# The pairs of four heads combined before the other four heads are chosen, in a fused encoder layer with retrieved experts

## The chip, the cores and the metric

The program runs on 1 core of one Trainium2 chip. The metric is the device time of one execution in microseconds (us). Three executions of the kernel before took 3947.78, 3959.03 and 3949.66 us; their median is 3949.66 us. Five engines work beside each other, each through its own list of instructions: PE multiplies matrices, DVE is the vector engine, ACT applies functions, POOL is GpSimd, and SP issues transfers. POOL issues the gathers.

## The reference, cut to what matters

One layer over 1024 tokens of width 1024: RWKV-7 time mixing and chunk-causal attention are added to `x`, then comes a product-key retrieval (PEER), then a gated input embedding and a last norm. The change lies in the retrieval:

```
q = (xb @ w_q).reshape(t, 8 heads, 2, 128)
s = einsum('thcd,hcnd->thcn', q, sub_keys)            # 128 scores for each half of each head
top_s, top_i = top_k(s, 16)                           # the choice: 16 of 128, twice for each head
cand_s = top_s[:, :, 0, :, None] + top_s[:, :, 1, None, :]       # 16 x 16 pairs
cand_i = top_i[:, :, 0, :, None] * 128 + top_i[:, :, 1, None, :]
best_s, best_pos = top_k(cand_s, 16)                  # 16 pairs of each head
idx  = take_along_axis(cand_i, best_pos)              # 8 heads x 16 = 128 experts of a token
gate = softmax(best_s)
act  = gelu(einsum('td,thkd->thk', xb, u_tab[idx]))
out  = einsum('thk,thkd->td', gate * act, v_tab[idx])
```

## The kernel before

The 1024 tokens are 8 blocks of 128 (a block's tokens lie on the 128 partitions), worked in 4 slices of two blocks. For each slice the program has `project_rwkv`, `rwkv` (a serial recurrence in chunks of 64 tokens), `project_rest`, `attend` and `select`. `select` (L753) forms the layer's sum, normalises it and multiplies with the query weights in 16 steps `i`, two for each head: ACT and POOL split a weight tile into two parts (L804, recorded as L282), PE multiplies (L806), PE multiplies with the keys (L813), ACT copies the scores to a tile `s` (L815, five buffers), and DVE chooses 16 of 128 for both blocks (`top16`, L821). After the 16 steps `combine` (L830) runs once for each of the two blocks, for all 8 heads: it adds the pairs of scores (`cs`, 9 instructions at L843) and of indices (`ci`, 11 instructions at L848), chooses 16 of the 50 pairs that can win (`top16` again), looks their indices up (`eq`, L864 to L867), writes the index tile `idx` in two halves of four heads (L869) and the softmax into `gate` (L871 to L876).

`gather` (L891) then works through the 128 experts of each token: for each `k`, POOL issues a gather of one row of `u` for each of the 128 tokens (L900, 128 rows of 4 KB), and DVE multiplies it with the token's input and sums (L902). Such an instruction on DVE is called a row product here; there are 1024 of them, 128 for each of the 8 blocks. In the first part of the program four buffers hold gathered rows (`row`, L882), later seven. The experts' second half is done for blocks 0 to 4 by a dense product over the whole table `v` (`expand` writes one-hot weights, `dense` multiplies) and for blocks 5 to 7 by gathers again (`add_rows`). `ple` and the last norm end the program.

No order is written out by hand. `everything` (L1064) gives each stage a number; a list scheduler fixes the order of each engine's list when the program is built, lower numbers first, by its own estimate of when operands are ready. `gather` has the numbers 50 to 53, most slices' stages lower ones, so row products fill places in which DVE would wait by that estimate. On the chip each engine keeps to that order.

Of the kernel before, what the change touches and what calls it, by code (L numbers as in the profile page):

```python
# [8 lines left out]
F = mybir.dt.float32  # L9
R = mybir.dt.float32r  # L10
I32 = mybir.dt.int32
# [140 lines left out]
class Program:  # L152
# [435 lines left out]
    def chunk_pre(self, pool, psum, B):  # L588
# [8 lines left out]
        halves = (slice(0, 64), slice(64, 128))  # L597
        G, V = [], []
        for c in range(2):
# [3 lines left out]
            for j in range(4):  # L603
# [10 lines left out]
                nc.scalar.activation(vs[:, j], ps[:, 384:448], AF.Copy)  # L614
            G.append(gs)
            V.append(vs)

        def level(l):
            m = t([128, 8, 64], "lm", 2)
            for c in range(2):  # L620
                self.aux.tensor_tensor(m[:, 4 * c:4 * c + 4], G[c][:, :, 0, 0:64],  # L621
                                       self.c("lmask")[:, None, l * 64:l * 64 + 64].to_broadcast([128, 4, 64]), op=OP.mult)
# [10 lines left out]
        for l in range(1, 6):  # L633
# [11 lines left out]
            nc.vector.tensor_tensor(xt, xt, d, op=OP.add)  # L645
        return G, V, xt

# [105 lines left out]
    def select(self, hf, side="left"):  # L753
        nc = self.nc
        bl = SLICES[hf]
        NB, N = len(bl), len(bl) * 128
        ts = self.tile(self.kp, [128, NB, 8, 2, 16], F, "ts", 1)
        ti = self.tile(self.kp, [128, NB, 8, 2, 16], U32, "ti", 1)
        with ExitStack() as s2:
            pool = self.pool(s2, "se", side)  # L760
            psum = self.pool(s2, "sp", side, True)
            t, bank = self.makers(pool, psum)
            y = t([128, 8, N], "act")
            for k in range(8):
                nc.sync.dma_start(y[:, k], self.yg[hf][k] if k < 4 else self.oT[hf][k - 4])
            xs = self.blocks(pool, self.rows("x"), bl)
            m = t([128, 8, N], "act")
            for d in range(8):
                ys = []
                for i, src in enumerate(("rw_wo", "mla_wo")):  # L770
                    w = self.weights(self.wp, self.I[src][d], 4)
                    ps = bank([128, N])
                    self.mm(ps, w, (y[:, 4 * i:4 * i + 4],), 4)
                    gt = t([128, N], "gate", 4)
                    nc.sync.dma_start(gt, self.zT[hf][20 + 8 * i + d])
                    nc.vector.tensor_tensor(gt, gt, ps, op=OP.mult)
                    ys.append(gt)
                self.aux.tensor_tensor(m[:, d], ys[0], ys[1], op=OP.add)
            acc = [bank([128, 512], *(("mm",) if i < 3 else ("tr", 1))) for i in range(2 * NB)]
            for k in range(8):  # L780
                w = self.tile(self.wp, [128, 8, 128], F, "w", WBUF).rearrange("p a n -> p (a n)")
                nc.sync.dma_start(w, self.I["w_out"][k * 128:k * 128 + 128])
                for b in range(NB):
                    for n in range(2):
                        nc.tensor.matmul(acc[2 * b + n], m[:, k, b * 128:b * 128 + 128], w[:, n * 512:n * 512 + 512],  # L785
                                         start=k == 0, stop=k == 7)
            for b, x in enumerate(xs):
                for n in range(2):
                    xd = x[:, n * 512:n * 512 + 512]
                    nc.vector.tensor_tensor(xd, xd, acc[2 * b + n], op=OP.add)  # L790
            for b, x in zip(bl, xs):
                nc.sync.dma_start(self.x1[b], x)
            gf = t([128, 8, N], "act").rearrange("p a b -> p (a b)")[:, :D]
            nc.sync.dma_start(gf, self.I["gffn"].to_broadcast([128, D]))
            rs = self.row_rstd(pool, xs, "n")
            for b, x in zip(bl, xs):
                nc.vector.scalar_tensor_tensor(x, x, rs[:, b - bl[0]:b - bl[0] + 1], gf, op0=OP.mult, op1=OP.mult)
                nc.sync.dma_start(self.h2[b], x)
            hT = [t([128, 8, N], "act", 2, R) for _ in range(2)]
            self.to_T(bank, xs, hT)  # L800
            for i in range(16):
                raw, = self.weights(self.wp, self.I["w_q"][i], 8)
                w = [t([128, 8, 128], n, 1, R) for n in (("whi", "wlo") if i % 2 == 0 else ("x0", "x1"))]
                self.split_to(w, raw, nc.gpsimd)  # L804
                ps = bank([128, N])
                self.mm(ps, w, hT, 8)  # L806
                q = t([128, N], "gate", 4)
                nc.scalar.activation(q, ps, AF.Copy)
                keys = t([128, 128], "keys", 3)
                nc.sync.dma_start(keys, self.I["keys"][:, i])  # L810
                ps = bank([128, NB, 128], "tr", 1)
                for b in range(NB):
                    nc.tensor.matmul(ps[:, b], q[:, b * 128:b * 128 + 128], keys, start=True, stop=True)  # L813
                s = t([128, NB, 128], "s", 5)
                nc.scalar.activation(s, ps, AF.Copy)  # L815
                for b in range(NB):
                    self.top16(s[:, b], ts[:, b, i // 2, i % 2], ti[:, b, i // 2, i % 2])
        for b in range(NB):
            self.combine(bl[b], self.kp, ts[:, b], ti[:, b])

    def top16(self, s, v, i):  # L821

# [4 lines left out]
        nc.vector.max(v[:, 8:16], s)  # L827
        nc.vector.max_index(i[:, 8:16], v[:, 8:16], s)

    def combine(self, b, xp, ts, ti):  # L830


        nc = self.nc
        G = 8
        t = lambda shape, tag, dt=F: self.tile(xp, shape, dt, tag, 1)
        tif = t([128, G, 2, 16], "tif")
        nc.vector.tensor_copy(tif, ti)
        cs, ci = t([128, G, 50], "cs"), t([128, G, 50], "ci", I16)
        o = 0
        bc = lambda x, n: x if x.shape[2] == n else x.to_broadcast([128, G, n])  # L840
        for i0, i1, j0, j1 in [(i, i + 1, 0, 16 // (i + 1)) for i in range(8)] + [(8, 16, 0, 1)]:
            n = (i1 - i0) * (j1 - j0)
            nc.vector.tensor_tensor(cs[:, :, o:o + n], bc(ts[:, :, 0, i0:i1], n), bc(ts[:, :, 1, j0:j1], n), op=OP.add)  # L843
            o += n
        o = 0
        for i0, i1, j0, j1 in RUNS:
            n = (i1 - i0) * (j1 - j0)
            nc.vector.scalar_tensor_tensor(ci[:, :, o:o + n], bc(tif[:, :, 0, i0:i1], n), 128.0,  # L848
                                           bc(tif[:, :, 1, j0:j1], n), op0=OP.mult, op1=OP.add)
            o += n  # L850
        bs, bp = t([128, G, 16], "bs"), t([128, G, 16], "bp", U32)
        idx = self.idx[b] = self.tile(self.sel, [128, 128], I32, f"idx{b}", 1)
        gate = self.gate[b] = self.tile(self.sel, [128, 128], F, f"gate{b}", 1)
        idf = t([128, G, 16], "idf")
        iv = idx.rearrange("p (g k) -> p g k", k=16)
        for g in range(G):
            self.top16(cs[:, g], bs[:, g], bp[:, g])
            for k0, n, m in ((0, 20, 4), (8, 50, 2)):
                if (g + 1) % m:
                    continue  # L860
                hs, ks = slice(g + 1 - m, g + 1), slice(k0, k0 + 8)
                sh = [128, m, 8, n]
                eq = self.tile(xp, [128, D], I16, "eq", 1)[:, :m * 8 * n].rearrange("p (g k n) -> p g k n", g=m, k=8)
                nc.vector.tensor_tensor(eq, bp[:, hs, ks, None].to_broadcast(sh),  # L864
                                        self.c("cand")[:, None, None, :n].to_broadcast(sh), op=OP.is_equal)
                nc.vector.tensor_tensor(eq, eq, ci[:, hs, None, :n].to_broadcast(sh), op=OP.mult)
                nc.vector.tensor_reduce(idf[:, hs, ks], eq, axis=AX.X, op=OP.add)  # L867
            if g % 4 == 3:
                nc.vector.tensor_copy(iv[:, g - 3:g + 1], idf[:, g - 3:g + 1])  # L869
        gv = gate.rearrange("p (h k) -> p h k", k=16)  # L870
        nc.vector.tensor_tensor(gv, bs, bs[:, :, 0:1].to_broadcast([128, G, 16]), op=OP.subtract)  # L871
        nc.scalar.activation(gv, gv, AF.Exp)
        sm = t([128, G], "sm")
        nc.vector.tensor_reduce(sm, gv, axis=AX.X, op=OP.add)
        nc.vector.reciprocal(sm, sm)
        nc.vector.tensor_tensor(gv, gv, sm[:, :, None].to_broadcast([128, G, 16]), op=OP.mult)  # L876
# [244 lines left out]
```

## Time and profile before

| | us |
|---|---|
| median of three executions | 3949.66 (3947.78 to 3959.03) |
| the profiled execution | 3942.72, span of its instructions 3940.7 |
| DVE busy | 3193.8 (81%) |
| PE busy | 3087.6 (78%) |
| POOL busy | 2050.4 (52%) |
| ACT busy | 1276.9 (32%) |

The profile is of one execution; times in it count from its first instruction. An engine's busy time says how long it worked, the waits say what ended its idle times, and the 40 digits of a line show the busy share of equal slices of the span, in tenths. A mean over the whole span mixes stages with different limits, so the stages are read one by one, in windows.

### The profile page before, as it was taken

To read this page: it belongs to the slowest core of one execution; us is meant where nothing else is said; L and a number is where in the kernel's file an instruction comes from. 1 tells how busy PE (TensorE), PEld (TensorE's weight loads), DVE (VectorE), ACT (ScalarE), POOL (GpSimd) and SP (SyncE) were. 2 spreads that over 40 slices of the span, in tenths; PEclk is the share of its full clock that TensorE was granted. 3 is DMA by queue.
4 is the path that set the end of the run, shared out by engine and by line. 5 is a ranking of instruction groups with operands and counts; after the bars stand their busy time and mean duration, and the time that the engine had idled before them with its cause. 6 is when DMAs were issued, how large, how long until landed. Compare 5 with 4: busy or idle time off the path is not lost.

```text
span 3940.7 us, 62191 instructions
## 1 busy us (share of the span) xinstructions
PE 3087.6 (78%) x21999; PEld 2517.8 (64%) x21999; DVE 3193.8 (81%) x6931; ACT 1276.9 (32%) x2723; POOL 2050.4 (52%) x1638
## 2 busy tenths in 40 slices
PE   7998778678879794878866687568888889989581
PEld 7885767666668673578735567446666667767351
DVE  2532888767899685899878778998999999999997
ACT  3231222133222174222138867522221222222341
POOL 0201456645654533576454425446767776666754
PEclk9998899888989796888967788779999999999796
DMA  6236598899868998878888998799999999999986
GB/s 200 88 112 200 183 321 286 285 318 309 313 188 309 322 323 285 305 243 279 311 276 284 302 336 274 233 321 341 386 384 371 390 379 372 373 385 352 329 279 232
DMA packets 502327, 1160.48 MB, mean 294 GB/s; under 512 B 54016, under 2 KB 228352, under 8 KB 502016
## 3 DMA queue, kind: packets, MB, share of 16 engines
q0 software_dynamic: 202752, 738.29, 52.7%
q1 hardware_dynamic: 281984, 402.48, 30.3%
q10 hardware_dynamic: 17280, 15.74, 1.2%
q8 instruction: 174, 2.85, 0.3%
q14 instruction: 137, 1.12, 0.1%
HBM read 1071.38 MB, written 84.93 MB: 293 GB/s over the span
## 4 chain that ended last, share of the span: by engine, by line
DVE 23%; PE 23%; issue 20%; DMA 17%; POOL 10%; ACT 5%; SPq 2%; POOLq 0%; DVEq 0%; ACTq 0%
DVE u L902 9%; DMA u<-in_u_dram,idx 9%; PE mm L290 7%; POOL u L900 6%; POOL u L915 4%; PE mm L785 2%; DVE oa L959 2%; PE w L961 1%; PE inv L586 1%; PE acc L997 1%; DMA u<-in_v_dram,idx 1%; DMA raw<-zT 1%; PE acc L998 1%; PE mm L292 1%; SPq L964 1%
## 5 line engine op out<-in xcount | busy, mean ns | idle before, releaser
L900 POOL DMA_INDIRECT u<-in_u_dram,idx x1024 | 1230.5, 1202 | 1182.1 <-DVE dots L902 625.2
L902 DVE CUSTOM_DVE_ANT_0 u<-u,gh 128x1024 f32<-128x1024 f32 x1024 | 1320.8, 1303 | 226.8 <-DMA u<-in_u_dram,idx 210.1
L915 POOL DMA_INDIRECT u<-in_v_dram,idx x384 | 485.7, 1265 | 230.6 <-DVE x L917 104.1
L290 PE MATMUL mm<-hT,w 128*128 128x128 f32 x4608 | 568.4, 284 | 11.8 <-DMA raw<-zT 3.5
L997 PE MATMUL acc<-vlo,Whi 128*128 128x512 f32 x1280 | 521.8, 408 | 67.4 <-DVE vlo L282 66.8
L290 PEld LDWEIGHTS mm<-hT,w 128*128 128x128 f32 x4608 | 553.1, 199 | 27.6 <-ACT z L326 7.8
L998 PE MATMUL acc<-vhi,Wlo 128*128 128x512 f32 x1280 | 513.4, 401 | 0.0
L996 PE MATMUL acc<-vhi,Whi 128*128 128x512 f32 x1280 | 374.3, 402 | 101.8 <-ACT vhi L280 83.0
L996 PEld LDWEIGHTS acc<-vhi,Whi 128*128 128x128 f32 x1280 | 244.9, 193 | 176.5 <-ACT vhi L280 93.1
L997 PEld LDWEIGHTS acc<-vlo,Whi 128*128 128x128 f32 x1280 | 248.4, 194 | 147.1 <-DVE vlo L282 96.7
L917 DVE SCALAR_TENSOR_TENSOR x<-u,gate,x 128x1024 f32<-128x1024 f32 x256 | 329.2, 1286 | 6.0 <-DMA u<-in_v_dram,idx 2.1
L280 ACT ACTIVATE vhi<-vr 128x512 fp32r<-128x512 f32 x256 | 158.8, 628 | 532.2 <-DMA vr<-in_v_dram 347.6
L961 PE MATMUL w<-ob,oa 128*128 128x128 f32 x1280 | 225.3, 334 | 98.1 <-ACT ob L955 53.5
L961 PEld LDWEIGHTS w<-ob,oa 128*128 128x128 f32 x1280 | 203.6, 240 | 124.9 <-ACT ob L955 81.6
L998 PEld LDWEIGHTS acc<-vhi,Wlo 128*128 128x128 f32 x1280 | 249.1, 195 | 51.6
L959 DVE TENSOR_SCALAR oa<-cst,pt 128x128 f32<-128x128 f32 x640 | 210.7, 388 | 39.3 <-PE w L961 34.8
L954 ACT ACTIVATE ob<-cst,pt 128x128 f32<-128x128 f32 x640 | 204.3, 396 | 0.6 <-PE w L961 0.5
L282 DVE TENSOR_TENSOR vlo<-vr,vhi 128x512 fp32r<-128x512 f32 x256 | 174.7, 693 | 8.0 <-ACT vhi L280 7.9
L280 ACT ACTIVATE Whi<-wr 128x1280 fp32r<-128x1280 f32 x64 | 81.5, 1273 | 287.0 <-PE acc L997 257.6
L917 DVE SCALAR_TENSOR_TENSOR gh<-u,gate,gh 128x1024 f32<-128x1024 f32 x128 | 167.9, 1311 | 4.9 <-DMA u<-in_v_dram,idx 3.0
L290 PE MATMUL mm<-act,w 128*128 128x256 f32 x512 | 134.0, 417 | 45.2 <-DMA act<-yg 29.1
L621 POOL TENSOR_TENSOR lm<-gs,cst 128x256 f32<-128x256 f32 x96 | 100.1, 1063 | 100.9 <-DVE gs L612 56.6
(331 smaller groups left out, 5511.6 us busy)
## 6 DMA issues: line engine op xcount, KB each, us to landing
w<-in_w_in_dram SPq DMA_DIRECT2D x144, 512.0 KB
vr<-in_v_dram SPq DMA_DIRECT2D x256, 256.0 KB
W<-ws SPq DMA_DIRECT2D x40, 1024.0 KB
wr<-W SPq DMA_DIRECT2D x64, 640.0 KB
w<-in_w_q_dram SPq DMA_DIRECT2D x64, 512.0 KB
w<-in_w_out_dram SPq DMA_DIRECT2D x32, 512.0 KB
u<-in_u_dram,idx POOLq DMA_INDIRECT x1024, 6.9
x<-in_x_dram SPq DMA_DIRECT2D x16, 512.0 KB
```

The lines of the kernel that those rows point to most:

```text
L280: self.nc.scalar.activation(act[0], x, AF.Copy)
L290: mm(ps, w[0][:, i], a[0][:, i], start=first, stop=last)
L900: nc.gpsimd.indirect_dma_start(out=u[:], out_offset=None, in_=self.I["u"], in_offset=bass.IndirectOffsetOnAxis(ap=idx[:, k:k + 1], axis=0))
L902: nc.vector.tensor_tensor_reduce(out=u[:], in0=u[:], in1=h[:], scale=1.0, scalar=0.0, op0=OP.mult, op1=OP.add, accum_out=dots[:, k:k + 1])
L915: nc.gpsimd.indirect_dma_start(out=v[:], out_offset=None, in_=self.I["v"], in_offset=bass.IndirectOffsetOnAxis(ap=idx[:, k:k + 1], axis=0))
L917: nc.vector.scalar_tensor_tensor(x, v, gate[:, k:k + 1], x, op0=OP.mult, op1=OP.add)
L954: nc.scalar.activation(c[:, i], self.c("iota"), AF.Abs, bias=pt[:, 1, k + i:k + i + 1])
L959: nc.vector.tensor_scalar(a, self.c("iota"), pt[:, 0, k:k + 1], pt[:, 2, k:k + 1], op0=OP.is_equal, op1=OP.mult)
L961: nc.tensor.matmul(ps[:, i], a, c[:, i], start=True, stop=True)
L996: nc.tensor.matmul(acc[b], wh, vh, start=i == 0, stop=False)
L997: nc.tensor.matmul(acc[b], wh, vl, start=False, stop=False)
L998: nc.tensor.matmul(acc[b], wl, vh, start=False, stop=i == G - 1)
```

## The change

`combine` handles four heads at a call instead of eight. It is called twice in each `select`: after step `i` = 7 for heads 0 to 3 of both blocks, and after step 15 for heads 4 to 7. Both calls write parts of the same `idx` and `gate` tiles.

```diff
@@ select
                 nc.scalar.activation(s, ps, AF.Copy)
                 for b in range(NB):
                     self.top16(s[:, b], ts[:, b, i // 2, i % 2], ti[:, b, i // 2, i % 2])
-        for b in range(NB):
-            self.combine(bl[b], self.kp, ts[:, b], ti[:, b])
+                if i % 8 == 7:
+                    hs = slice(i // 2 - 3, i // 2 + 1)
+                    for b in range(NB):
+                        self.combine(bl[b], self.kp, ts[:, b, hs], ti[:, b, hs], hs)
@@ combine
-    def combine(self, b, xp, ts, ti):
+    def combine(self, b, xp, ts, ti, heads):
...
-        G = 8
+        G = 4
...
-        idx = self.idx[b] = self.tile(self.sel, [128, 128], I32, f"idx{b}", 1)
-        gate = self.gate[b] = self.tile(self.sel, [128, 128], F, f"gate{b}", 1)
+        if b not in self.idx:
+            self.idx[b] = self.tile(self.sel, [128, 128], I32, f"idx{b}", 1)
+            self.gate[b] = self.tile(self.sel, [128, 128], F, f"gate{b}", 1)
+        idx, gate = self.idx[b], self.gate[b]
         idf = t([128, G, 16], "idf")
-        iv = idx.rearrange("p (g k) -> p g k", k=16)
+        iv = idx.rearrange("p (g k) -> p g k", k=16)[:, heads]
...
-        gv = gate.rearrange("p (h k) -> p h k", k=16)
+        gv = gate.rearrange("p (h k) -> p h k", k=16)[:, heads]
```

Lines behind L818 stand 2 to 4 lines lower in the changed kernel (the gather is L904, the row product L906, the write of the indices L873). In the order of the engines the whole list behind the first `select` is made anew. Three places are shown.

DVE at the first row product of the program, before: the first half of block 0's indices is written (L869), and the first row products (L902, written to `u` and `dots`) stand between the look-ups (`eq`, `idf`) of the remaining heads.

```order
L869 CAST idx_995_4356<-idf_4358 128x64
L864 TENSOR_TENSOR eq_4402<-bp_4355,cst_60 128x800
L866 TENSOR_TENSOR eq_4402<-eq_4402,ci_4333 128x800
L867 TENSOR_REDUCE idf_4358<-eq_4402 128x2x8
L864 TENSOR_TENSOR eq_4416<-bp_4355,cst_60 128x640
L902 ISA u_4535,dots_4534<-u_4535,gh_4532 128x1024
```

The same place after the change (L873 writes the indices, L906 is the row product; `s_4352`, `s_4402` and `s_4452` are the scores of the last three steps, `bp` and `cs` belong to block 1's first heads):

```order
L873 CAST idx_931_3954<-idf_3956 128x64
...
L826 MAX ts_3218<-s_4452 128x8 x2
L829 MAX bs_4020<-cs_3998 128x8 x4
L829 MAX ts_3218<-s_4352 128x8 x2
L828 MATCH_REPLACE s_4402<-ts_3218,s_4402 128x128 x2
L827 MAX_INDEX ti_3219<-ts_3218,s_4452 128x8 x2
L830 MAX_INDEX bp_4021<-bs_4020,cs_3998 128x8 x4
L875 TENSOR_TENSOR gate_944_4023<-bs_4020 128x64
L830 MAX_INDEX ti_3219<-ts_3218,s_4352 128x8 x2
L829 MAX ts_3218<-s_4402 128x8 x2
L906 ISA u_4601,dots_4600<-u_4601,gh_4598 128x1024
L828 MATCH_REPLACE s_4452<-ts_3218,s_4452 128x128 x2
```

The first row product now stands among the last choices from 128 scores, in front of the end of three of them; before, all choices lay ahead of it.

POOL at its first gather, after the change: the two splits of the last two steps (`wlo`, `x`), and behind them the gathers.

```order
L282 TENSOR_TENSOR x_992_4317<-w_4314,x_991_4316 128x1024
L282 TENSOR_TENSOR wlo_4367<-w_4364,whi_4366 128x1024
L282 TENSOR_TENSOR x_1008_4417<-w_4414,x_1007_4416 128x1024
L904 DMA u_4601<-in_u_dram,idx_931_3954 128x1024
L904 DMA u_4604<-in_u_dram,idx_931_3954 128x1024
```

Before, the same place reads alike with L900: in both lists all 16 splits of the first `select` stand ahead of the first gather, so nothing moved there.

DVE in the recurrence of the second slice, at the end of its last chunk but one (`us` and `hs` are steps of a chunk, `H` its state), before:

```order
L663 COPY us_7087<-seq_7078 128x256
L902 ISA u_1155_4933,dots_4923<-u_1155_4933,gh_4921 128x1024
...
L902 ISA u_4936,dots_4923<-u_4936,gh_4921 128x1024
...
L667 TENSOR_TENSOR hs_7106<-seq_7089,H_7031 128x256
L902 ISA u_4939,dots_4923<-u_4939,gh_4921 128x1024
...
L669 TENSOR_TENSOR H_7108<-hs_7106,er_6279 128x256
```

and after the change:

```order
L663 COPY us_7153<-seq_7144 128x256
L906 ISA u_5026,dots_4989<-u_5026,gh_4987 128x1024
...
L906 ISA u_5029,dots_4989<-u_5029,gh_4987 128x1024
...
L667 TENSOR_TENSOR hs_7172<-seq_7155,H_7097 128x256
L669 TENSOR_TENSOR H_7174<-hs_7172,er_6345 128x256
```

One row product fewer stands between the same steps. Over the whole list of DVE, the number of row products that stand ahead of the same instruction is counted from the two orders:

| instruction on DVE | its start before, us | row products ahead, before | after |
|---|---|---|---|
| last choice of the first `select` begins | 440 | 0 | 0 |
| first mixing step of the second slice's `rwkv` | 559 | 34 | 54 |
| last query product of its `project_rest` | 682 | 81 | 99 |
| first mask of the second `attend` | 820 | 140 | 146 |
| first choice of the second `select` | 1072 | 230 | 238 |
| first indices of the second slice written | 1191 | 256 | 256 |
| last query product of the third slice | 1278 | 288 | 294 |
| first gated product of the third `select` | 1565 | 396 | 407 |
| first choice of the third `select` | 1708 | 441 | 449 |
| last query product of the fourth slice | 1938 | 519 | 523 |
| first gated product of the fourth `select` | 2279 | 656 | 662 |
| first choice of the fourth `select` | 2421 | 693 | 700 |
| first addition of `dense` | 2630 | 741 | 750 |

## Rows read from the trace of the kernel before

**Rows 1.** The page: engines' busy time, slices of the span, the chain.
```profile
PE 3087.6 (78%) x21999; PEld 2517.8 (64%) x21999; DVE 3193.8 (81%) x6931; ACT 1276.9 (32%) x2723; POOL 2050.4 (52%) x1638
...
DVE 2532888767899685899878778998999999999997
...
DVE 23%; PE 23%; issue 20%; DMA 17%; POOL 10%; ACT 5%; SPq 2%; POOLq 0%; DVEq 0%; ACTq 0%
```

**Rows 2.** Stretches: length, each engine's busy time and instructions, clock, DMA.
```profile
core 0: us, PE busy (x) PEld busy (x) DVE busy (x) ACT busy (x) POOL busy (x), PEclk, DMA share, GB/s
387.00:417.00 30.00, 28.44 (x231) 27.68 (x232) 19.84 (x130) 13.34 (x26) 19.98 (x9) 1.00 0.51 159
417.00:443.00 26.00, 20.32 (x166) 19.56 (x164) 19.48 (x133) 8.23 (x17) 11.18 (x5) 1.00 0.40 134
443.00:518.00 75.00, 56.64 (x464) 54.00 (x464) 71.36 (x261) 12.83 (x29) 27.50 (x24) 0.84 0.75 276
518.00:559.00 41.00, 21.64 (x157) 20.06 (x158) 27.61 (x57) 14.54 (x31) 20.19 (x19) 0.79 0.88 303
...
682.00:820.00 138.00, 90.38 (x1265) 79.80 (x1259) 94.93 (x170) 22.48 (x44) 81.50 (x73) 0.79 0.84 284
...
1072.00:1278.00 206.00, 172.68 (x1809) 155.76 (x1810) 198.50 (x644) 49.04 (x95) 105.77 (x83) 0.93 0.75 248
...
1708.00:1938.00 230.00, 191.13 (x2088) 173.53 (x2085) 225.06 (x684) 56.16 (x106) 143.98 (x106) 0.90 0.82 274
...
2421.00:2630.00 209.00, 120.38 (x711) 108.26 (x709) 202.44 (x682) 97.82 (x224) 88.74 (x66) 0.76 0.80 262
2630.00:3171.00 541.00, 476.51 (x1952) 370.99 (x1951) 503.93 (x812) 121.67 (x167) 371.09 (x277) 0.97 0.98 371
```

**Rows 3.** Combining in order of time on DVE: start, length of all, count.
```profile
444.44 1.27 DVE L848 SCALAR_TENSOR_TENSOR ci<-tif 128x64 int16<-128x64 f32 x11
```

**Rows 4.** Line L843: count, shortest/median/longest in ns.
```profile
L843 DVE TENSOR_TENSOR cs<-ts x72: 149/181/439, 440.3 to 2561.5; 128x16 f32<-128x16 f32 x24, 128x64 f32<-128x64 f32 x16, 128x40 f32<-128x40 f32 x8, 128x32 f32<-128x32 f32 x8
```

**Rows 5.** Lines by group, 443 to 518 us: busy, mean ns, idle before.
```profile
L900 POOL DMA_INDIRECT u<-in_u_dram,idx x22 | 25.4, 1154 | 57.0 <-DVE idx L869 29.7 <-DVE dots L902 25.8 <-issue 1.2
L902 DVE CUSTOM_DVE_ANT_0 u<-u,gh 128x1024 f32<-128x1024 f32 x19 | 24.0, 1266 | 3.2 <-DMA u<-in_u_dram,idx 3.2
```

**Rows 6.** POOL in order of time, around its first gather.
```profile
430.76 2.40 POOL L282 TENSOR_TENSOR x<-w,x 128x1024 fp32r<-128x1024 f32 x1
462.88 1.62 POOL L900 DMA_INDIRECT u<-in_u_dram,idx  x1 [29.72 <-DVE idx L869]
```

**Rows 7.** Tile `u`, 682 to 820 us: instructions, idle times, landing.
```profile
L902 DVE CUSTOM_DVE_ANT_0 u<-u,gh x60: 1205/1225/1737, 681.1 to 818.3; 128x1024 f32<-128x1024 f32 x60
...
  DVE dots L902: 42.0, 25
  DMA u<-in_u_dram,idx: 35.7, 29
...
DMA to landing us min/median/max: 5.1/5.8/7.8
```

**Rows 8.** Tile `u`, 1278 to 1565 us.
```profile
L902 DVE CUSTOM_DVE_ANT_0 u<-u,gh x109: 1194/1221/1269, 1276.8 to 1559.1; 128x1024 f32<-128x1024 f32 x109
...
  DMA u<-in_u_dram,idx: 45.9, 42
```

**Rows 9.** Tile `u`, 1938 to 2279 us.
```profile
L902 DVE CUSTOM_DVE_ANT_0 u<-u,gh x139: 1149/1218/2602, 1937.5 to 2278.9; 128x1024 f32<-128x1024 f32 x139
...
  DMA u<-in_u_dram,idx: 46.9, 47
```

**Rows 10.** Line L872: table loads for the softmax's exponential on ACT.
```profile
L872 ACT ACT_TABLE_LOAD  x6: 1283/1283/1283, 451.2 to 2542.0; - x6
```

**Rows 11.** POOL in order of time, between blocks 1 and 2.
```profile
1153.98 0.94 POOL L900 DMA_INDIRECT u<-in_u_dram,idx  x1 [0.30 <-DVE ts L824]
...
1191.36 1.48 POOL L900 DMA_INDIRECT u<-in_u_dram,idx  x1 [17.91 <-DVE idx L869]
```

## The prediction

> **What bounds the kernel now.** I read the page first: which engine is busy, and in which part of the span. DVE is busy for 3193.8 us, more than any other engine, and its digits stand between 5 and 9 from the fifth slice on, and at 8 or 9 from the 25th to the last but one [rows 1]. The chain that ended last is shared by DVE, PE and transfers, so no single engine explains the whole span. So I went on to windows, cut where the order of DVE has a landmark that both kernels share (the table of the change). The reader is to see three kinds of stretch. Around each choice and combination DVE has next to no idle time: 198.5 of 206 us from 1072, 225.1 of 230 from 1708, 202.4 of 209 from 2421 [rows 2]. In the dense stage from 2630 DVE is busy for 503.9 of 541 us while the transfers stand at a share of 0.98 [rows 2]. Between them lie stretches in which DVE has idle time and yet paces the others, since row products stand in its list in front of the recurrence's steps: from 682 to 820 us DVE is busy for 94.9 of 138 us [rows 2], waits 29 times and 35.7 us for a gathered row, while POOL waits 42.0 us for DVE to free a buffer [rows 7]. Each waits for the other, as a ring of four buffers does when a row lands 5.8 us after its issue [rows 7].
>
> So the question for the change is: what DVE work does it add, which idle time of DVE does it fill, and how many row products are left when the dense stage begins.
>
> **What is added.** A call of `combine` has 1 + 9 + 11 instructions for the pairs and 4 for the softmax that cover all its heads at once; the choices and look-ups go by head or by groups of heads, and their number stays. So each block pays 25 more instructions on DVE, with half the columns each: 200 in all. Their price is read where such instructions follow each other: the 11 of L848 take 1.27 us together [rows 3]. They have 400 columns; at the rate of a row product, 1.22 us for 1024 columns [rows 7], that is 0.48 us, which leaves 0.79 us, or 72 ns for each instruction. 25 x 0.072 = 1.8 us a block, 3.6 us a slice, 14.4 us in all. The other bound is the recorded length: the shortest of L843 lasts 149 ns [rows 4], which makes 3.7 us a block, 30 us in all. I take 14.4, since lengths overlap when instructions follow closely, and the row of eleven shows it. Nothing below 14.4 is to be had, except where DVE is idle.
>
> The Trainium skill, VectorE: DVE Perf Modes, in the section on the errata, gives two fixed terms: 58 cycles in its table, and about 150 cycles as measured, at 0.96 GHz; by my estimate from that page these are 60 and 156 ns for each instruction. The row of eleven agrees with the first and the recorded lengths with the second; by the second, 25 x 8 x 0.156 = 31 us would be added and the sum below would end 17 us higher.
>
> The eight further softmaxes put at most eight more table loads of 1.28 us on ACT [rows 10]; ACT is busy for 49 of 206 us beside the second combination [rows 2], so I cost them at nothing; without that cover DVE would wait for them, up to 10 us.
>
> **What is moved.** In the first `select` DVE is idle for 10.2 us in the first eight steps (19.84 of 30 us busy) and 6.5 us in the last eight (19.48 of 26) [rows 2]. Combining both blocks takes 71.4 us less 24.0 us of row products, so 47 us [rows 2, 5]; a quarter of it, with its 0.9 us of additions, is 12.7 us. In the new order the first indices stand behind some 14 of the 16 steps' choices (39.3 us of DVE work for 16, so 2.46 each) and one and a half such quarters: 387 + 10 + 14 x 2.46 + 19 = about 450 us, against 462.9 [rows 6]. So the gathers begin about 13 us earlier, not by the 26 us of the last eight steps and more. POOL is free for it: its last split ended at 433.2 [rows 6]. Of the 6.5 us of idle time I count all as filled; of the 17 us between 443 and 559 none, since behind the combination the new order has the same rows as the old one.
>
> **The sum, stretch by stretch.** A row product costs 1.22 us of DVE [rows 7 to 9]. Where DVE waits for rows, one more or less also moves its share of those waits: 35.7 us over 59 products from 682 to 820, so 1.82 us each; 45.9 over 109 from 1278, so 1.64; 46.9 over 139 from 1938, so 1.56 [rows 7 to 9]. The numbers of products between landmarks are differences in the table.
> - 387 to 559: 20 more, 24.4 + 3.6 - 6.5 = +21.5 us.
> - 559 to 682: 2 fewer, -2.4.
> - 682 to 820: 12 fewer (47 for 59) at 1.82, -21.8. Bounds: at 1.22 it is -14.6; if the ring alone paces, at 138 / 59 = 2.34, it is -28.1. The recurrence and PE (busy 90 of 138 us [rows 2]) leave room for either; the waits of DVE stand between.
> - 820 to 1072: 2 more, +2.4. 1072 to 1278: 2 fewer and the second slice's additions, +1.2.
> - 1278 to 1565: 5 more at 1.64, +8.2. 1565 to 1708: 3 fewer, -3.7.
> - 1708 to 1938: 4 fewer and additions, -1.3.
> - 1938 to 2279: 2 more at 1.56, +3.1. 2279 to 2421: 1 more, +1.2.
> - 2421 to 2630: 2 more and additions, +6.0.
>
> So `dense` begins 14.4 us later, with 9 more rows done. In the dense stage one row is worth between 1.22 us of DVE and, at 371 GB/s [rows 2], 524 KB or 1.41 us of transfer; 9 x 1.32 = 11.9 us come back. The sum is +2.5 us. On the profiled execution's own time that is 3942.72 + 2.5 = 3945.2 us. That execution lies 6.9 us under the median of the runs shown, so I forecast 3949.66 + 2.5 = 3952 us: **no change that can be measured**. About 0.3%, 12 us, is what a measurement of this kernel can tell from none.
>
> In words: the early start is real but short, most of it is spent on combining twice, and from the second slice on both halves of the heads meet a DVE without idle time. Between blocks 1 and 2 POOL stands from 1154 to 1191 us for want of indices [rows 11], and the new order leaves such a gap: 256 row products stand ahead of the second slice's first indices in both lists.
>
> The bounds: least, if all 17 us of idle time from 443 to 559 are filled and the ring alone paces from 682, 2.5 - 17 - 6.3 = -21; most, if no idle time is filled (+6.5), the thinned stretch gives 1.22 a product (+7.2), the additions cost their recorded lengths (+15.4) and the 5 products from 1278 cost the stretch's whole pace of 287 / 108 = 2.66 (+5), 2.5 + 34 = +37.
>
> The Trainium skill, DMA: Bandwidth & Descriptors, in the section Anatomy of one DMA, fits 2.0 us plus bytes / 436 GB/s to such a transfer: for 524 KB, by my estimate, 3.2 us. The trace does not agree, 5.8 us and more at a loaded machine [rows 7]; at 3.2 us four buffers would keep DVE supplied, no product would wait, and all would count 1.22 us: the sum would be +7 us, no other forecast.
>
> **The rivals.**
> - *The whole early start is kept, faster.* The 20 row products among the combinations hide the latency of their rows, and the waits up to 559 us go: 2.5 - 17 = -14.5 us, 3935 us. For it: in the old order 19 row products among look-ups waited only 3.2 us [rows 5]. Against it: the rows behind the combination stand as before.
> - *DVE stands at the first row product, slower.* It now stands in front of the end of three choices and of block 1's first heads. On POOL its gather stands behind all 16 splits, and a split waits for PE, which waits for a free score tile, which waits for DVE's choices that now stand behind combining. If the gather goes out at 463 as before, the 13 us are lost to a wait on DVE: 2.5 + 13 = +15.5 us, 3965 us. It decides from a wait of some 10 us for rows or scores before 460 us. Against it: five score tiles, and 30 us between POOL's last split and first gather now [rows 6].
> - *Each added instruction costs its recorded length, slower.* The mechanism is that a dependent instruction waits for the whole of the one before: 200 x 0.149 = 30 us for 14.4, so +18 us, 3967 us. Against it stands the row of eleven, which read one tile and do not wait for each other. The second of the skill's two terms is this rival's rule.
> - *The change does not do what it says:* if a gather of the first heads waited for the write of the last ones, which go to the same tile, the lead would be nothing. In the old kernel the first gather left 0.3 us behind the first half's indices [rows 5, 6], with the second half still to come, so I give this nothing of its own.
>
> **How the numbers follow.** No change 0.46; whole start kept 0.27; first row product 0.16; recorded lengths 0.11. The last two end on the slower side: faster by over 0.3% 0.27, within it 0.46, slower 0.27. The range holds the three outer cases, 3935, 3965 and 3967, with about half of what the bounds of -21 and +37 leave beyond them: 3931 to 3976 us.
>
> **What would show it.** The first gather on POOL should start at about 450 us. The mean of the combining instructions should show 25 more a block, with DVE's busy time up by 15 to 30 us, since recorded lengths overlap. From 682 us on, in the stretch up to the second `attend`, DVE's waits for rows should fall by some 7 us and the stretch by some 20. The first addition of `dense` should start near 2645 us, with 750 row products done, and the last row product should end 2 or 3 us later than now. It is wrong if `dense` begins before 2636 or after 2655 us, or if a wait on DVE of more than 10 us at one row product stands in the first `select`.

## The result and the profile after

| | before | after |
|---|---|---|
| median of seven executions, us | 3951.70 (3944.41 to 3962.84) | 3976.10 (3970.16 to 3985.05) |
| ratio after / before | | 1.0059, 95% interval 1.0041 to 1.0077 |
| span of the profiled execution, us | 3940.7 | 3973.8 |
| DVE busy, instructions | 3193.8, 6931 | 3208.8, 7131 |
| span less DVE busy | 746.9 | 765.0 |

The changed kernel is slower by 0.59%, 16 to 30 us by the interval. The forecast was 3952 us and no change that can be measured: a slower result had a chance of 0.27, and the time lies at the upper end of the range (3976). The two profiles differ by 33 us and not by 24, since the one of before was a quick execution, 9 us under its median.

The page of the changed kernel, with the lines that answer to [rows 1], and the row of the row product:

```profile
PE 3105.8 (78%) x21999; PEld 2527.8 (64%) x21999; DVE 3208.8 (81%) x7131; ACT 1292.9 (33%) x2741; POOL 2085.8 (52%) x1638
...
DVE  2532878767899685899879778989989999999997
...
DVE 24%; PE 22%; issue 20%; DMA 17%; POOL 12%; ACT 4%; SPq 2%; POOLq 0%; DVEq 0%; ACTq 0%
...
L906 DVE CUSTOM_DVE_ANT_0 u<-u,gh 128x1024 f32<-128x1024 f32 x1024 | 1305.8, 1288 | 224.1 <-DMA u<-in_u_dram,idx 199.1
```

DVE has 200 instructions and 15.0 us more. The sum had 14.4, but the two agree by luck. If a time in which two records overlap counts for the earlier one, combining takes 220.5 us of DVE in place of 184.8, so 35.7 more; row products take 18.4 us less and all the rest 2.3 less. And the time beside it did not fall: 18.1 us more of the span has no DVE instruction.

Windows of the changed kernel, cut at the same landmarks as [rows 2] (columns as there):

```profile
421.00:464.00 43.00, 22.05 (x163) 21.28 (x161) 43.00 (x237) 9.90 (x20) 14.85 (x9) 0.82 0.33 101
464.00:601.00 137.00, 78.32 (x599) 74.23 (x600) 108.69 (x306) 27.85 (x61) 71.38 (x59) 0.76 0.88 304
...
719.00:832.00 113.00, 89.71 (x1362) 80.33 (x1358) 82.47 (x152) 21.92 (x43) 73.65 (x60) 0.83 0.87 291
1088.00:1298.00 210.00, 179.07 (x1873) 162.10 (x1872) 199.60 (x691) 53.12 (x100) 110.11 (x83) 0.92 0.73 248
1734.00:1965.00 231.00, 186.44 (x1898) 168.62 (x1897) 223.99 (x730) 54.23 (x101) 128.37 (x98) 0.87 0.78 260
2441.00:2668.00 227.00, 131.57 (x746) 116.58 (x745) 214.64 (x752) 108.06 (x251) 97.18 (x71) 0.74 0.80 264
2668.00:3210.00 542.00, 475.76 (x1932) 370.64 (x1933) 499.75 (x807) 120.02 (x164) 377.43 (x276) 0.96 0.98 367
```

From 421 to 464 us, where the first heads are combined among the last choices, DVE has no idle time at all. The stretch 719 to 832 us is 25 us shorter than its counterpart, the last combination (2441 to 2668) 18 us longer.

Where the 33 us came from, by the starts of the landmark instructions in both traces, less the 3.6 us by which the first choice already started later (391.14 for 387.53), beside the sum:

| stretch (times of before) | row products | forecast | measured |
|---|---|---|---|
| 387 to 559 | +20 | +21.5 | +38.6 |
| 559 to 820 | -14 | -24.2 | -30.9 |
| 820 to 1278 | 0 | +3.6 | +8.9 |
| 1278 to 1565 | +5 | +8.2 | +16.8 |
| 1565 to 1708 | -3 | -3.7 | -11.6 |
| 1708 to 2421 | -1 | +3.0 | -5.5 |
| 2421 to 2630 | +2 | +6.0 | +18.4 |
| 2630 to 3181, the last row product | -9 | -11.9 | -11.6 |
| 3181 to the end | 0 | 0 | +6.3 |

### What stands in the first stretch

DVE in order of time in the changed kernel, the longest groups of the first heads' combining:

```profile
417.43 2.38 DVE L845 TENSOR_TENSOR cs<-ts 128x16 f32<-128x16 f32 x2
419.99 2.52 DVE L845 TENSOR_TENSOR cs<-ts 128x8 f32<-128x8 f32 x4
...
424.32 3.27 DVE L850 SCALAR_TENSOR_TENSOR ci<-tif 128x32 int16<-128x32 f32 x11
...
433.99 2.65 DVE L845 TENSOR_TENSOR cs<-ts 128x64 f32<-128x64 f32 x7
...
441.10 1.75 DVE L880 TENSOR_TENSOR gate<-gate,sm 128x64 f32<-128x64 f32 x1
443.17 2.82 DVE L868 TENSOR_TENSOR eq<-bp,cst 128x640 int16<-128x640 uint32 x1
```

Two additions of 16 columns take 2.38 us, and the eleven of the indices 3.27 us with half the columns of the eleven that took 1.27 [rows 3]. POOL over the same time:

```profile
417.30 2.38 POOL L282 TENSOR_TENSOR wlo<-w,whi 128x1024 fp32r<-128x1024 f32 x1 [2.38 <-ACT whi L280]
419.83 2.40 POOL L282 TENSOR_TENSOR x<-w,x 128x1024 fp32r<-128x1024 f32 x1
424.60 2.42 POOL L282 TENSOR_TENSOR wlo<-w,whi 128x1024 fp32r<-128x1024 f32 x1 [2.38 <-ACT whi L280]
433.57 2.46 POOL L282 TENSOR_TENSOR x<-w,x 128x1024 fp32r<-128x1024 f32 x1 [6.55 <-ACT x L280]
440.39 2.38 POOL L282 TENSOR_TENSOR wlo<-w,whi 128x1024 fp32r<-128x1024 f32 x1 [4.35 <-ACT whi L280]
442.91 2.40 POOL L282 TENSOR_TENSOR x<-w,x 128x1024 fp32r<-128x1024 f32 x1
458.84 1.14 POOL L904 DMA_INDIRECT u<-in_u_dram,idx  x1 [13.53 <-DVE cs L828]
```

Each long group overlaps a split of the query weights, and ends some 0.1 to 0.7 us behind it: the product for `gate` begins at 441.10 and ends at 442.85, the split ends at 442.77. A DVE instruction with two inputs in the memory stands here while POOL's runs. Before, the last split ended at 433.2 and combining began at 440 [rows 4, 6]. The Trainium skill, SBUF — State Buffer, in the section SBUF: two separate sides, says of such a pair that whichever starts first holds a shared pair of ports for its whole instruction and the other is blocked; the rows agree.

The splits themselves come later than before, with waits of 6.55 and 4.35 us for ACT: the last ends at 445.31 us. POOL then stands for 13.53 us until DVE, which combines and chooses in turns, has written the first indices (L873, at 458.36). So the first gather starts at 458.84 us, only 4 us ahead of [rows 6]; 450 was forecast.

DVE's waits for gathered rows between the first gather and slice 2's first mixing step, after (464 to 601 us) and before (464 to 559 us), with their sum, number and longest:

```profile
DVE u L906 <- DMA u<-in_u_dram,idx: 20.2, 11, 4.4
```

```profile
DVE u L902 <- DMA u<-in_u_dram,idx: 11.8, 8, 3.7
```

By the same count the +38.6 us of this stretch are 13.3 of combining (the sum had 3.6), 22.6 of row products (24.4), 3.2 of idle time (-6.5) and -0.5 of all else. In the idle time the waits for scores fell by 8.0 us, from 16.1 to 8.1, and the waits for rows rose by 8.4.

The next slice's load also moved. The last choice of the first `select` on DVE, in the changed kernel:

```profile
473.14 0.30 DVE L830 FIND_INDEX8 ti<-ts,s 128x8 uint32<-128x128 f32 x1
```

and SP's load of slice 2's `x` behind it, which takes the memory of the finished `select`:

```profile
473.52 0.81 SPq L239 DMA_DIRECT2D x<-in_x_dram  x2
```

Before, it was issued at 443.73 us. PE's first instruction for slice 2 follows at 500.30 us in place of 458.42. This was not in the prediction.

Tile `u` from 719 to 832 us, the counterpart of [rows 7]:

```profile
L906 DVE CUSTOM_DVE_ANT_0 u<-u,gh x49: 1150/1224/1896, 718.1 to 831.8; 128x1024 f32<-128x1024 f32 x49
...
  DVE dots L906: 29.1, 16
  DMA u<-in_u_dram,idx: 23.5, 18
```

The waits for rows fell by 12.2 us here, more than the 7 forecast.

### The profile page after: what moved, and what is told of

Its sections match the earlier page's. It is cut to its first block, busy times and chain, and to the rows that moved or that the text cites. A ratio compares the mean times of both kernels' runs of the same rounds, so it can differ in the third digit from the quotient of the medians.

```text
span 3973.8 us, 62414 instructions
## 1 busy us (share of the span) xinstructions
PE 3105.8 (78%) x21999; PEld 2527.8 (64%) x21999; DVE 3208.8 (81%) x7131; ACT 1292.9 (33%) x2741; POOL 2085.8 (52%) x1638
## 4 chain that ended last, share of the span: by engine, by line
DVE 24%; PE 22%; issue 20%; DMA 17%; POOL 12%; ACT 4%; SPq 2%; POOLq 0%; DVEq 0%; ACTq 0%
DMA u<-in_u_dram,idx 10%; DVE u L906 9%; PE mm L290 8%; POOL u L919 5%; POOL u L904 5%; DVE oa L963 2%; PE mm L785 2%; PE inv L586 1%; PE w L965 1%; DMA W<-ws 1%; ACT ob L958 1%; PE mm L292 1%; SPq L968 1%; PE mm L293 1%; PE mm L294 1%
## 5 line engine op out<-in xcount | busy, mean ns | idle before, releaser
L904 POOL DMA_INDIRECT u<-in_u_dram,idx x1024 | 1270.4, 1241 | 1157.9 <-DVE dots L906 611.5
L906 DVE CUSTOM_DVE_ANT_0 u<-u,gh 128x1024 f32<-128x1024 f32 x1024 | 1305.8, 1288 | 224.1 <-DMA u<-in_u_dram,idx 199.1
L965 PEld LDWEIGHTS w<-ob,oa 128*128 128x128 f32 x1280 | 200.5, 237 | 140.2 <-ACT ob L959 83.5
```

The lines of the kernel that those rows point to most:

```text
L904: nc.gpsimd.indirect_dma_start(out=u[:], out_offset=None, in_=self.I["u"], in_offset=bass.IndirectOffsetOnAxis(ap=idx[:, k:k + 1], axis=0))
L906: nc.vector.tensor_tensor_reduce(out=u[:], in0=u[:], in1=h[:], scale=1.0, scalar=0.0, op0=OP.mult, op1=OP.add, accum_out=dots[:, k:k + 1])
L965: nc.tensor.matmul(ps[:, i], a, c[:, i], start=True, stop=True)
```

## The experiments

Twelve kernels. "Idle" is the span less DVE's busy time of the profiled execution; the ratio is to the kernel before, which ran beside them (medians 3949.64 to 3954.30 us). A profiled execution can lie 15 us off its kernel's median: that of e3_first is the quickest of twelve (3924.98 us), that of e6_after_x the slowest (3981.07).

| run | median, us | ratio, 95% interval | DVE busy | idle |
|---|---|---|---|---|
| e1_late4 | 3985.02 | 1.0071 (1.0050 to 1.0092) | 3201.5 | 785.5 |
| e2_low | 3969.32 | 1.0043 (1.0027 to 1.0060) | 3217.4 | 748.4 |
| e3_first | 3939.70 | 0.9965 (0.9951 to 0.9979) | 3191.0 | 732.0 |
| e4_rest | 3960.54 | 1.0023 (1.0004 to 1.0042) | 3196.5 | 769.3 |
| e7_after_hold3 | 3976.69 | 1.0049 (1.0031 to 1.0067) | 3212.1 | 760.3 |
| e8_before_hold3 | 3962.63 | 1.0033 (1.0020 to 1.0046) | 3204.5 | 747.4 |
| e9_before_hold1 | 4010.72 | 1.0141 (1.0126 to 1.0156) | 3175.2 | 839.9 |
| e11_no_lo | 3971.01, one run | | 3209.7 | 759.5 |
| e12_after_nolo4 | 3903.32 | 0.9879 (0.9854 to 0.9905) | 3156.1 | 749.2 |
| e13_before_nolo4 | 3878.77 | 0.9819 (0.9791 to 0.9846) | 3135.7 | 746.1 |
| e6_after_x | 3966.34 | 1.0047 (1.0030 to 1.0064) | 3230.9 | 748.3 |
| e14_first_x | 3954.83 | 1.0009 (0.9993 to 1.0026) | 3205.0 | 756.2 |

### Which select, and which order

```diff
 e1_late4 (of the changed kernel), behind the 16 steps
+        for hs in (slice(0, 4), slice(4, 8)):
+            for b in range(NB):
+                self.combine(bl[b], self.kp, ts[:, b, hs], ti[:, b, hs], hs)
 e2_low (put back to rank behind the call)
+                    if i == 7: self.tc.cur_priority = rank + 5000
 e3_first (G = the heads of the call)
-                if i % 8 == 7:
+                if i % 8 == 7 and (hf == 0 or i == 15):
 e4_rest
-                if i % 8 == 7:
+                if i % 8 == 7 and (hf > 0 or i == 15):
```

> Theory A (the 200 added DVE instructions make the loss): both halves are combined behind the last choice, so the same 200 instructions are added and no choice is delayed; then the loss stays, +14 to +23 us against the kernel before (which is at 3951.7 us). Theory B (the last choice of the first select is held back by about 21 us, the load of the next slice's x waits for it, and PE stands idle until then): the load of x is issued at 444 to 448 us as before, the first mixing step of slice 2 is within 10 us of 558.5 us, and the kernel is at 0 to +10 us against before.

> The early calls stay, with a lower rank than every choice of the same select, so that they fill idle time of DVE alone. Theory A: as the changed kernel, +14 to +23 us against before. Theory B: the load of x goes back to 444 to 450 us, slice 2's first mixing step to within 12 us of before, and the kernel to 0 to +10 us against before.

> Early halves in the first select alone; the other three combine eight heads at once, with 50 instructions added in place of 200. Theory A: a quarter of the loss, +4 to +6 us against before. Theory B: the load of x is issued at 470 to 475 us, the first mixing step comes 35 to 45 us later than before, and most of the loss stays, +12 to +22 us.

> The reverse: the first select as before, early halves in the other three, 150 instructions added. Theory A: three quarters of the loss, +10 to +17 us against before. Theory B: the load of x at 444 us, and the loss that is not made in the first select alone, 0 to +10 us.

The first two did not do what they were made for. A call that is written behind the 16 steps, or ranked below them, still fills DVE's time between choices, since the scheduler looks at what is ready: the first gathers start at 456.4 and 456.7 us, and the load of x at 464.2 and 464.5 us. They are two more lists with the same instructions, at 1.0071 and 1.0043, so 28 and 17 us above the kernel before, beside 23 for the changed kernel.

The third goes against both theories: with halves in the first `select` alone the load of x is nearly as late (469.6 us) and slice 2's first mixing step too (595.4 us), and yet the kernel is 0.35% *faster* than before. With halves in the other three it is 0.23% slower, 9 us, with the load of x at 446.0 us; taken alone this fits theory B and lies just under theory A's range. The two do not add up to +0.59%: by the ratios, halving the first `select` gains 14 us in the one list and costs 14 in the other, and halving the later ones costs 9 us beside an unhalved first and 37 beside a halved one. The time that combining takes on DVE does not tell the two apart: by the count above it rises by 28.2 us in the first case and by 20.3 in the second.

### Row products in the recurrences

Theory C came from [rows 7 to 9]: 138 us for 59 products, 287 for 108. If the ring of buffers paces these stretches, fewer products there should pay.

```diff
 e7, e8 (gather of block 3 called behind the third select; e9: block 1, second select, held for its first choice)
             nc.sync.dma_start(h, self.h2[b])
+            if b == 3:
+                nc.vector.tensor_tensor(h[:, 0:1], h[:, 0:1], self.late, op=OP.add)
...
                     nc.vector.tensor_tensor(gt, gt, ps, op=OP.mult)
+                    if hf == 2 and d == 0 and i == 0:
+                        self.late = self.tile(self.kp, [128, 1], F, "late", 1)
+                        nc.vector.tensor_scalar(self.late, gt[:, 0:1], 0.0, None, op0=OP.mult)
```

> The changed kernel, with the row products of block 3 held until the first gated product of the third select: up to there 384 of them stand in DVE's list in place of 407, and 733 in place of 750 ahead of dense; the list up to 1298 us is the same. Theory C (in the recurrences the ring of four buffers sets the pace, so a row product there costs 2.3 to 2.6 us, against 1.3 in dense, and the change is slower since its list puts more of them there): the third select's first gated product comes 50 to 60 us earlier than in the changed kernel, dense begins 40 us earlier, and the time falls by 17 x (2.5 - 1.3) = 20 us, to 3950 to 3960 us. Rival (the slices' own steps set the pace and the row products only fill): the products come out of the filled time, the time stays or rises by up to 22 us, 3976 to 3998 us.

> The same hold in the kernel before: 384 row products in place of 396 ahead of the third select, 731 in place of 741 ahead of dense. Theory C: the third select about 30 us earlier, the time 12 us lower, 3938 to 3945 us. Rival: no change or up to 13 us slower.

> The kernel before with block 1's row products held until the first choice of the second select: 128 in place of 230 ahead of it, 327 in place of 396 ahead of the third select, 691 in place of 741 ahead of dense. Theory C, if the price of 2.3 us holds down to so few: dense begins 115 us earlier, and 50 x (2.3 - 1.3) = 50 us come off, about 3900 us. Rival (a floor is reached where the slice's own steps set the pace, and row products would have been hidden there): dense begins less than 65 us earlier and the kernel is slower than before, up to 4017 us.

Theory C falls: the times are 3976.69, 3962.63 and 4010.72 us where it wanted 3950 to 3960, 3938 to 3945 and about 3900, and all three are as the rival had them. Windows from the last query product of the third slice to the first gated product of its `select`, in the changed kernel and in e7, whose lists are the same up to there but for the held products:

```profile
1298.00:1602.00 304.00, 221.00 (x1557) 177.81 (x1555) 209.02 (x501) 151.82 (x375) 141.00 (x117) 0.79 0.91 303
```

```profile
1296.00:1573.00 277.00, 207.60 (x1542) 170.49 (x1540) 177.24 (x445) 141.11 (x355) 110.24 (x93) 0.84 0.87 292
```

27 us for 23 products is 1.17 us each, not 2.6; e8 gives 0.71. In e9 the whole `attend` of slice 2 has no product at all; before and e9:

```profile
820.00:1072.00 252.00, 215.10 (x1608) 162.39 (x1606) 191.99 (x391) 78.02 (x168) 141.16 (x119) 0.89 0.92 317
```

```profile
819.00:1023.00 204.00, 190.37 (x1250) 143.10 (x1250) 77.78 (x205) 76.31 (x167) 26.48 (x23) 0.92 0.53 157
```

48 us for 90 products, 0.53 each, and PE is then busy for 190 of 204 us: more than half of a product's 1.22 us is hidden there. What is put off costs more at the end. From the first addition of `dense` to the end of the span it is 1310.6 us with 283 products left (before), 1332.4 with 291 (e7), 1400.9 with 333 (e9): 1.8 us each between the first and the last. The average pace of a stretch is not the price of one more instruction in it.

### The splits beside the combining

```diff
 e11 (hf == 0 and i > 7), e12 and e13 (i > 7 in every select)
-                self.split_to(w, raw, nc.gpsimd)
+                if hf == 0 and i > 7:
+                    nc.scalar.activation(w[0], raw, AF.Copy)
+                    w = [w[0], w[0]]
+                else:
+                    self.split_to(w, raw, nc.gpsimd)
```

> The changed kernel without POOL's eight splits of the last eight steps in the first select (the high part of the weights stands for the low one: the low part's products are left out). Theory: the added and sums instructions of two inputs stand beside a POOL split for some 2 us each time; without the splits the eleven of the first heads take 1.0 to 1.3 us in place of 3.27, and the first gather starts 8 to 12 us earlier, at 447 to 451 us. Rival (they wait for choices they read): lengths and first gather stay within 3 us, 456 to 459 us.

DVE in e11, the same six groups as above:

```profile
419.15 0.24 DVE L849 TENSOR_TENSOR cs<-ts 128x16 f32<-128x16 f32 x2
419.56 0.42 DVE L849 TENSOR_TENSOR cs<-ts 128x8 f32<-128x8 f32 x4
...
421.98 1.06 DVE L854 SCALAR_TENSOR_TENSOR ci<-tif 128x32 int16<-128x32 f32 x11
...
430.03 0.74 DVE L849 TENSOR_TENSOR cs<-ts 128x64 f32<-128x64 f32 x7
...
435.34 0.22 DVE L884 TENSOR_TENSOR gate<-gate,sm 128x64 f32<-128x64 f32 x1
435.99 0.82 DVE L872 TENSOR_TENSOR eq<-bp,cst 128x640 int16<-128x640 uint32 x1
```

and POOL's first gather:

```profile
451.99 1.13 POOL L908 DMA_INDIRECT u<-in_u_dram,idx  x1 [43.30 <-DVE cs L832]
```

3.50 us in place of 15.39. The first gather comes at 452.0 us (447 to 451 expected), and from the first choice to slice 2's first mixing step it is 195.3 us in place of 209.6: +24.4 us to before, where +21.5 was forecast and +38.6 measured. So leaving out the splits takes away 14 of the 17 us by which this stretch was missed. Combining makes 10.9 of the 14 (49.4 us of DVE in place of 60.3, and 47.0 before); the rest is shorter waits and one row product less. The splits do not hold up this stretch in the kernel before: without them (e13, below) it lasts 173.6 us there, with two row products more, and with them 171.0. That the time hardly fell (3971.01 us, a single run) raised the next question: is this the loss?

> The changed kernel without POOL's splits of the last eight query steps in all four selects (the high part of the weights stands for the low one, whose products are so left out). Theory D (the first heads' combining now runs beside POOL's splits, and its two-input instructions stand there; before, no combining did): combining takes DVE 30 to 38 us in each select in place of 48, 44, 41 and 34, and the time against the kernel before with the same part left out (the next run) is +0 to +8 us, in place of +23. Rival (the added instructions and the new list make the loss, the splits do not): the difference of the two stays at +18 to +28 us.

> The same part left out of the kernel before, as the other side of that comparison. Theory D: its combining stays at 28 to 35 us a select, since no split lay beside it; its time falls only by what row products and choices lost beside those splits, 5 to 25 us, to 3928 to 3948 us. Rival: as much faster as the changed kernel without them.

It is not. Without these splits the changed kernel still is 3903.32 - 3878.77 = 24.6 us slower than its counterpart, as with them (24.4). The busy times of e12 and of e13:

```profile
PE 3068.1 (79%) x21999; PEld 2505.8 (64%) x21999; DVE 3156.1 (81%) x7131; ACT 1295.4 (33%) x2741; POOL 1982.8 (51%) x1606
```

```profile
PE 3088.3 (80%) x21999; PEld 2509.1 (65%) x21999; DVE 3135.7 (81%) x6931; ACT 1281.9 (33%) x2727; POOL 1995.2 (51%) x1606
```

Here DVE's busy time is 20.4 us apart and the idle time 3.1. Combining takes 200.5 us in e12 and 187.0 in e13, by the count above: the 200 instructions cost DVE 13.5 us without these splits, close to the 14.4 of the sum, and 35.7 with them. Theory D was wrong about the kernel before: it lost as much to its splits, since its row products of the later selects stood beside them. Leaving out 32 splits took 58.1 us off its DVE, and 52.7 off that of the changed kernel. With the change, combining stands beside splits where row products stood; by the pages' rows the row products of the whole program are 15.0 us shorter in sum (1305.8 for 1320.8).

### The late load of the next slice

```diff
 e6 (of the changed kernel), e14 (of e3_first)
-            xp = self.pool(s2 if hf == 2 else s3, "x", side)
+            xp = self.pool(s2 if hf == 2 else s3, "x", "right" if hf == 1 else side)
```

> The changed kernel with the x tiles of slice 2 at the other end of the memory, so that their load need not wait for the last choice of the first select. Theory B: the load is issued before 400 us in place of 473, slice 2's first mixing step comes at 570 to 585 us in place of 601, and of that 5 to 15 us last to the end, 3961 to 3971 us. Rival (the late load is covered, as the 31 us that come back by 820 us say): 3972 to 3980 us.

> The two edits together that look best: halves in the first select alone (3939.7 us), and slice 2's x tiles at the other end of the memory. Theory B: 5 to 15 us faster than without the move, 3925 to 3935 us. Rival: 3936 to 3944 us.

SP in e6:

```profile
283.24 0.81 SPq L239 DMA_DIRECT2D x<-in_x_dram  x2
315.40 0.91 SPq L239 DMA_DIRECT2D x<-in_x_dram  x2
```

The load left early and the first mixing step came at 582.5 us in place of 600.7. At the third slice's last query product the kernel is level with the changed one again (1299.8 and 1298.3 us); but this profile is of the slowest of e6's twelve executions, so how much was lost by then it does not settle. The median, 3966.34 us, lies in theory B's range. By the ratios, 1.0047 and 1.0059, the gain is 5 us, and their intervals overlap: it is not shown, and not excluded. The late load is not where most of the 23 us went: e3_first has it as well and is faster than the kernel before. On e3_first the same edit, which should have helped or done nothing, cost 17 us by the ratios (3954.83 us).

## Why the prediction was right in its range and wrong in its sum

Its forecast of no change that can be measured failed, and by its own sign it was wrong: `dense` began at 2668.5 us, behind the 2655 that it named. That the range still reaches the time is luck, since its upper end came from rivals whose mechanisms did not show.

- **The step that failed: the price of the added and moved combining.** The working took each instruction at the length it had where it stood, and did not ask what POOL does at the new place. [Rows 6] showed it: splits up to 433 us, of 2.40 us each. Combining took 35.7 us more of DVE, not 14.4.
- **The price without POOL: right.** 72 ns each was worked out from [rows 3]; the eleven of e11, with half the columns, take 1.06 us: 0.24 us for 200 columns less leaves 0.82, or 75 ns each. Between e13 and e12 the 200 instructions cost 13.5 us of DVE, 68 ns each. The rival of recorded lengths, 3967 us, came nearer to the time, but by a mechanism that the rows refute.
- **The stretch 387 to 559: mis-sized,** +21.5 for +38.6. Without the splits it comes out at +24.4, and the first gather at 452.0 for 450. "POOL is free for it" was read at the old place: in the new list the last split ended at 445.3 us, not at 433.2.
- **"I count all as filled": right, but not kept.** DVE's wait for score copies in the first `select` fell by 8.0 us, and the waits for rows from 682 to 820 us by 12.2. The sum let both stand as gains to the end. In the first stretch the waits for rows gave back 8.4 us, and DVE's idle time over the program is 746.9 us before and 765.0 after (9 of the 33 us between the two profiles are the quick execution of before). In nine of the twelve runs, with `dense` begun up to 118 us apart (2569.1 and 2687.5), it lies between 746 and 770 us.
- **The later selects: the sign right, the size not.** Three comparisons halve them and change nothing else in the source: by the ratios +9 us (e4 to before), +37 (changed kernel to e3) and +15 (e6 to e14). The sum gave 10.8 us for their instructions.
- **Dense: right to its last row product** (-11.6 for -11.9), with +6.3 us behind it that the sum had at nothing.
- **First row product as a wait:** no wait of 10 us there; the longest for a row between 464 and 601 us is 4.4.

The cause of the whole 24 us stays open, and with it why the same edit costs 9 us in one list and 37 in another. The splits explain the first stretch and the time of combining, but without them the kernels are as far apart as with them. Every edit makes the whole list anew, and lists with the same work differ: the changed kernel, e1 and e2 lie 23, 28 and 17 us above the kernel before, and e14 lies 17 above e3, by ratios that are each known to 5 to 8 us. A scatter of 10 to 17 us between lists is about what the prediction called the limit of a measurement, 12 us; a sum of +2.5 us could not foretell the sign. In the pair e12 and e13 DVE's busy time makes 20.4 of the 23.5 us by which the spans differ, and combining 13.5 of that; for the pair before and after the two profiles put 15.0 us to busy and 18.1 to idle, and no run divides the latter further.

One rival was not tested: PE's granted clock, here a mean over the program as a share of full speed. It is 0.867 to 0.875 in the seven executions of the changed kernel and 0.872 to 0.886 in those of the kernel before that ran beside the experiments, and PE is busy for 18.2 us more with the same 21999 instructions. Whether the lower clock makes the program longer or follows from its waits is not shown. It is not the cause between e12 and e13: there the clock is 0.877 to 0.884 and 0.877 to 0.882, and PE's busy time is 20.2 us *shorter* in the slower kernel.

The fastest kernel that computes all of the reference is e3_first: early halves in the first `select`, where DVE has idle time and no row product is ready, and eight heads at a call in the other three. It is 0.35% (0.21 to 0.49) faster than the kernel before; that is 14 us, no more than the scatter between lists, so whether its placing or its list is the reason is not shown.

## What to carry to other kernels

Before work is moved on DVE, look at what POOL does at the new place, and price instructions with two inputs there by the end of POOL's instruction and not by their own length. Idle time that an early start fills is a gain only if the stretch that follows does not wait for something else: compare the idle time of the whole program, not of the stretch. Take the price of one more instruction in a stretch from two kernels that differ in it, since the stretch's mean pace can be several times as high; and where a scheduler makes the list anew, split an edit by its places, for one of them may gain what the others lose.

## What the runs showed of the hardware

- A POOL subtraction of 128 x 1024 (2.40 us) held DVE's two-input instructions until its end, even one of 64 columns: 1.75 us for 0.22. Leaving out 32 of them, 77 us of POOL's time, took 58 us off DVE and 71 us off the kernel before (e13, whose list is a new one too).
- The choices do not stand: in the kernel before, a MAX8 of 128 scores takes 272 ns alone and 276 beside POOL's arithmetic (medians of 192 and 64), while the 51 row products that begin beside it take 2068 ns on average, and the median of the others is 1216. Beside it means that the instruction begins more than 0.2 us before the end of one of POOL's.
- Such small instructions of two inputs are otherwise cheap in a row: eleven in 1.06 us, while each one's recorded length is 168 to 208 ns.
